# Prefill of a hybrid attention and mLSTM step: the norm half a block later, and four gated temporaries on the attention's probability tiles

## The chip, the cores and the metric

The kernel runs on one core of a Trainium2 chip. The metric is the device time of one execution in microseconds (us), the median over the runs. TensorE is called PE, VectorE DVE, ScalarE ACT, GpSimd POOL, and SyncE, whose queue issues most DMAs, SP.

## The reference, cut to what matters

One layer is applied to 128 prompt tokens and to 1024 latent tokens of width 1024. An attention group of 8 heads and an mLSTM group of 4 heads stand side by side, one output projection merges them, and a SwiGLU FFN follows. Each sub-layer begins with an RMS norm and ends in a gated addition to the residual:

```
mix = concatenate([attn_o, hm], axis=-1) @ w_out
x   = x + g1 * mix
h2  = rmsnorm(x, norm2_w) * (1 + sc2) + sh2
x   = x + g2 * (swiglu(h2, w_gu, w_down))
```

`hm` is the mLSTM's output, `g1`, `sc2`, `sh2` and `g2` come from the conditioning (one set for the prompt, one for the latents). A last RMS norm gives the two `y` outputs.

## The kernel before, in words

The 1152 tokens are 9 blocks of 128 (block 0 is the prompt), and three blocks make a chunk. Matrix products in float32 quality are made from three products of high and low parts (`whi`, `wlo` of a weight, `th`, `tl` of an activation).

The stages are: the conditioning and the input projection; the four mLSTM heads, with the attention of chunk 0 beside them; a stage called **prefill**; then the FFN of the three chunks, with the attention of the next chunk woven in beside the first products of each.

`prefill` works through the nine blocks. It multiplies the mLSTM half of `mix` with its half of `w_out` and adds the gated result to the residual. For each block `b` there are these steps:

- `mix(b)`: four transposes of the block's `hm` on PE, a copy on ACT (`th`, L1265) and a subtraction on DVE (`tl`, recorded as L141). It ends by issuing the load of `hm` of block `b + 2`.
- `half(b, n)`, for each half `n` of the 1024 columns: `out_block`, twelve 128x512 matmuls into one PSUM bank (L1219, L1221, L1223), and then `add_gated`: a multiplication of the bank with the gate on DVE into a temporary `t` (L1180), and an addition of `t` to the residual tile on POOL (L1181). Blocks 6 to 8 load `x` and store the sum instead (L1279 to L1283).
- `end(b)`: for blocks 0 to 2, `stats` (a squared sum on ACT, L1398, and a reciprocal square root in a dozen small DVE steps, L131 to L137), and, for `b` = 2, 3, 4, `norm2(0, cur, b - 2)`.

`norm2` makes the FFN's input of one block, in two halves: a scaled copy on ACT (`y`, L1414), four transposes on PE (L120), four scalings (one on ACT, L1422, three on DVE, L1424) into the tile `both`, a copy of the high part on ACT (L1429) and the low part on POOL (L141, `aTl`). `gate_up` of chunk 0 (L1435 to L1437) begins when the three blocks of chunk 0 are through this.

The temporary `t` has the tag `t2`, with three buffers, in the pool `ft`. That pool is opened after the pools of the mLSTM stage are closed. The attention's probabilities `pr` have a tag of their own with two buffers, in the pool `ap2`, which was opened before the attention of chunk 0; `both` of `norm2` uses the same tag.

PSUM banks for `mix`, `half` and `norm2` come from `bank()`: three buffers of one pool, and every fourth call the one buffer of another.

Every `yield` of `prefill` adds 0.35 to a counter, and at each full one a step of the attention of chunk 1 is issued: first the load and transposes of a block's queries, then one head after the other (scores `S` on PE, L1111; maximum on DVE, L1113; exponential into `pr` on ACT, L1114; high part `ph` on ACT, L1117; low part `pl` on DVE, L1118; two transposing DMAs; later the products with the values, L1135 and L1136). The step's PE work is tied behind the last matmul of the `half` that was issued before it:

```
with tc.issue_after(cur["gate"]), tc.issue_after(loaded["gate"]), tc.issue_after(loaded["hm"]), tc.issue_after(loaded["pe"]):
    next(att, None)
```

The order on each engine is not the program's: a scheduler places the instructions by their place in the program and by what is ready. `hot(n)` puts an instruction `n` places ahead; `norm2` stands under `hot(800)`, `stats` and the attention under `hot(200)`.

Of the kernel before, what the change touches and what calls it, by code (L numbers as in the profile page):

```python
# [8 lines left out]
F32 = mybir.dt.float32  # L9
# [10 lines left out]
P = 128  # L20
# [13 lines left out]
CB = 3  # L34
NCH = NB // CB
CT = CB * P
# [10 lines left out]
def hybrid_step(ctx: ExitStack, tc: tile.TileContext, I: dict, O: dict):  # L47
# [3 lines left out]
    dve = nc.vector  # L51
    pool = nc.gpsimd
# [3 lines left out]
    def hot(n):  # L56
        return tc.high_priority(n)

    def nm(s):
        uid[0] += 1  # L60
        return f"{s}_{uid[0]}"
# [19 lines left out]
    def xrow(b):  # L81
        if b == 0:
            return I["x_prompt"][0]
        return I["x_sample"][0, (b - 1) * P : b * P, :]
# [21 lines left out]
    def bank():  # L106
        turn_of[0] += 1
        at = psum["mm"] if "mm1" not in psum or turn_of[0] % 4 else psum["mm1"]
        return at.tile([P, 512], F32, name=nm("mm"), tag="mm")
# [9 lines left out]
    def transpose(out, in_, n=P):  # L119
        nc.tensor.transpose(out, in_, ident[:n, :n])  # L120
# [19 lines left out]
    def sub(out, full, hi, eng):  # L140
        (dve if eng == "dve" else pool).tensor_tensor(out=out, in0=full, in1=hi, op=ALU.subtract)  # L141
# [187 lines left out]
    ps = bank()  # L329
# [3 lines left out]
    ps = bank()  # L333
# [730 lines left out]
    ap2 = ctx.enter_context(tc.tile_pool(name="ap2", bufs=1, side="right", reuse_waits="tile"))  # L1064
# [88 lines left out]
    def a_tiles():  # L1153
        return (hp.tile([P, KD, CT], F32R, name=nm("aTh"), tag="b2"),
                hp.tile([P, KD, CT], F32R, name=nm("aTl"), tag="b3"))
# [18 lines left out]
    def t2():  # L1174
        return ft.tile([P, 512], F32, name=nm("t2"), tag="t2", bufs=3)

    def add_gated(x1, ps, g, n, eng=dve):
        cs = slice(n * 512, (n + 1) * 512)
        t = t2()
        dve.tensor_tensor(out=t, in0=ps, in1=g, op=ALU.mult)  # L1180
        eng.tensor_tensor(out=x1[:, cs], in0=x1[:, cs], in1=t, op=ALU.add)  # L1181

# [16 lines left out]
    def out_pieces(half, n, raw=None):  # L1199
        pieces = []  # L1200
        for j in range(2):
            r0 = half * 512 + 2 * j * P
            rows = w_out[r0 : r0 + 2 * P, n * 512 : (n + 1) * 512].rearrange("(a p) n -> p a n", p=P)
            pieces.append(load_piece([(full_view, rows)], (2, 512), raw=raw))
        return pieces

    def out_gates():
        gs = []
        for n in range(2):
            gl = xg.tile([P, 512], F32, name=nm("gl"), tag=("gl", "gx")[n], bufs=1)  # L1210
            dma(gl, g_d[0, 1:2, n * 512 : (n + 1) * 512].to_broadcast([P, 512]))
            gs.append(gl)
        return gs

    def out_block(ws, n, th, tl):
        ps = bank()
        for k in range(4):
            wh = ws[n][k // 2][0]
            mm(ps, th[:, k], wh[:, k % 2, :], start=(k == 0), stop=False)  # L1219
        for k in range(4):  # L1220
            mm(ps, th[:, k], ws[n][k // 2][1][:, k % 2, :], start=False, stop=False)  # L1221
        for k in range(4):
            loaded["pe"] = mm(ps, tl[:, k], ws[n][k // 2][0][:, k % 2, :], start=False, stop=(k == 3)).ins  # L1223
        return ps

    def prefill(cur, nxt):

        x1s = cur["x1"], nxt["x1"]
        cur["rs"] = []

        def load_hm(b):
            if b >= NB:
                return None
            hm = xe.tile([P, 512], F32, name=nm("hmr"), tag="hmr", bufs=2)
            if b < CB:
                loaded["hm"] = dma(hm, hm_d[0][b * P : (b + 1) * P, :]).ins
            else:
                r = dma(hm.rearrange("p (h n) -> p h n", n=P), hm_d[b // CB][:, :, b % CB * P : (b % CB + 1) * P])
                if b == CB:
                    loaded["hm"] = r.ins  # L1240
            return hm

        def load_x1(b):
            if CB <= b < 2 * CB:
                dma(x1s[1][b % CB], xrow(b))

        hms = hms_first
        ws = [ws_first]
        gs = out_gates()
        gx_all = xe.tile([P, D], F32, name="gx_all", tag="mx", bufs=3)  # L1250
        gate = loaded["gate"] = dma(gx_all, g_d[0, 0:1, :].to_broadcast([P, D])).ins
        ws.append(out_pieces(1, 1))
        cur["gate"] = loaded["piece"]
        gx = [gx_all[:, n * 512 : (n + 1) * 512] for n in range(2)]
        mixed = {}

        def mix(b):
            t = xe.tile([P, NQ, P], F32R, name=nm("mx"), tag="mx", bufs=3)
            th, tl = mixed[b] = t[:, 0:4], t[:, 4:8]
            hm = hms.pop(0)  # L1260
            ps = bank()
            for j in range(4):
                transpose(ps[:, j * P : (j + 1) * P], hm[:, j * P : (j + 1) * P])
            psv = ps.rearrange("p (j x) -> p j x", j=4)
            nc.scalar.copy(th, psv)  # L1265
            sub(tl, psv, th.bitcast(F32), "dve")
            with tc.issue_after(gate):
                hms.append(load_hm(b + 2))

        def half(b, n):  # L1270
            c, i = divmod(b, CB)
            cs = slice(n * 512, (n + 1) * 512)
            ps = out_block(ws, n, *mixed[b])
            g = gx[n] if b == 0 else gs[n]
            if c < 2:
                add_gated(x1s[c][i], ps, g, n, pool)
            else:
                xt = t2()
                dma(xt, xrow(b)[:, cs])  # L1279
                t = t2()  # L1280
                dve.tensor_tensor(out=t, in0=ps, in1=g, op=ALU.mult)
                pool.tensor_tensor(out=xt, in0=xt, in1=t, op=ALU.add)
                dma(x1_d[i][:, cs], xt)  # L1283

        def end(b):
            if b < CB:
                with hot(200):
                    cur["rs"] += stats(x1s[0][b : b + 1])
            if 2 <= b < CB + 2:
                yield from norm2(0, cur, b - 2)  # L1290

        for b in range(2):
            mix(b)
            yield
        for b in range(2):
            half(b, 0)
            yield
        load_x1(2)
        half(0, 1)
        yield  # L1300
        yield from end(0)
        load_x1(3)
        mix(2)
        yield
        half(1, 1)
        yield
        yield from end(1)
        for b in range(2, NB):
            load_x1(b + 2)
            half(b, 0)  # L1310
            yield
            if b + 1 < NB:
                mix(b + 1)
                yield
            half(b, 1)
            yield
            yield from end(b)

    def attn_out_first(oT, ready):

# [81 lines left out]
    def norm2(c, a, i):  # L1402

        x1 = a["x1"][i]
        if "h2" not in a:
            a["h2"] = a_tiles()
        th, tl = a["h2"]
        r = a["rs"][i]
        both = ap2.tile([P, KD, P], F32, name=nm("fl"), tag="pr", bufs=2)
        cnd = 0 if c * CB + i == 0 else 1  # L1410
        for half in range(2):
            with hot(800):
                y = fp.tile([P, 512], F32, name=nm("y"), tag="y", bufs=2)
                act(y, x1[:, half * 512 : (half + 1) * 512], AF.Copy, scale=r)  # L1414
                ps = bank()
                for j in range(4):
                    transpose(ps[:, j * P : (j + 1) * P], y[:, j * P : (j + 1) * P])
                full = both[:, half * 4 : half * 4 + 4]
                for j in range(4):
                    k = half * 4 + j  # L1420
                    if j == 0 and c == 0:
                        act(full[:, j, :], ps[:, j * P : (j + 1) * P], AF.Identity, scale=scale2[:, k, cnd : cnd + 1], bias=shift2[:, k, cnd : cnd + 1])  # L1422
                        continue
                    dve.tensor_scalar(  # L1424
                        out=full[:, j, :], in0=ps[:, j * P : (j + 1) * P],
                        scalar1=scale2[:, k, cnd : cnd + 1], scalar2=shift2[:, k, cnd : cnd + 1],
                        op0=ALU.mult, op1=ALU.add)
                oh = th[:, half * 4 : half * 4 + 4, i * P : (i + 1) * P]
                nc.scalar.copy(oh, full)  # L1429
                sub(tl[:, half * 4 : half * 4 + 4, i * P : (i + 1) * P], full, oh.bitcast(F32), "pool" if c == 0 else "dve")  # L1430
            yield True
# [141 lines left out]
    cur, nxt = {}, {}  # L1573
# [27 lines left out]
    for c in range(NCH):  # L1601
        if c + 1 < NCH:
# [17 lines left out]
            cur = nxt  # L1620
# [61 lines left out]
```

## Time and profile before

| | |
|---|---|
| time, median of 3 runs | 1529.1 us (1527.36 to 1534.01) |
| the profiled execution, own time | 1531.07 us |
| its span, first to last instruction | 1529.3 us |
| PE busy in the span | 1473.0 us (96%) |
| DVE, ACT, POOL busy | 1015.8, 770.4, 268.8 us |
| mean granted PE clock | 0.989 of full speed |
| prefill on PE, first `mix` to last `half` | 485.4 to 567.9 us |

The busy times are of one execution. What an engine does off the path that sets the end costs nothing; a stretch in which PE waits, or runs at a lower granted clock, is lost only if PE is the one that is waited for afterwards.

### The profile page before, as it was taken

What the parts mean: (1) busy time and instruction counts of PE and PEld (TensorE: products, weight loads), DVE (VectorE), ACT (ScalarE), POOL (GpSimd) and SP (SyncE); (2) the same over time, 40 slices, a digit from 0 to 9 for tenths busy, and PEclk for the clock granted to TensorE, in tenths of its full rate; (3) what the DMA queues carried; (4) which work ended last, traced back from release to release, by engine and by line L of the source; (5) the groups of instructions that cost most, each with busy time, mean ns of one, the idle gap of its engine ahead of it and who ended that gap; (6) DMA issues with size and microseconds to landing.
All of it is one profiled execution on the core that took longest, in us unless ns stands there. A gap on an engine that the chain in (4) does not pass through costs nothing.

```text
span 1529.3 us, 23410 instructions
## 1 busy us (share of the span) xinstructions
PE 1473.0 (96%) x8539; PEld 1244.7 (81%) x8539; DVE 1015.8 (66%) x2025; ACT 770.4 (50%) x1429; POOL 268.8 (18%) x354
## 2 busy tenths in 40 slices
PE   6899999999998899999999999999999999999997
PEld 3545567677766789999898999989998989999996
DVE  4887654838568866878637587787866585554554
ACT  4764475947654645556433444656553443323333
POOL 0113423333344441010010100100010101101110
PEclk9899999999999999999999999999999999999998
DMA  9664323523456577869635357886864445544541
GB/s 359 205 198 147 101 71 42 120 53 62 110 177 207 135 180 187 200 156 195 171 115 166 124 184 212 198 184 145 201 145 138 138 139 179 158 135 126 153 144 56
DMA packets 387113, 233.77 MB, mean 153 GB/s; under 512 B 170102, under 2 KB 347462, under 8 KB 386998
## 3 DMA queue, kind: packets, MB, share of 16 engines
q1 hardware_dynamic: 385006, 228.69, 55.0%
q10 hardware_dynamic: 1864, 3.20, 0.9%
q8 instruction: 67, 1.10, 0.3%
q14 instruction: 48, 0.39, 0.1%
q0 software_dynamic: 128, 0.39, 0.1%
HBM read 182.21 MB, written 11.69 MB: 127 GB/s over the span
## 4 chain that ended last, share of the span: by engine, by line
PE 78%; DVE 5%; DMA 3%; ACT 3%; issue 1%; POOL 1%; SPq 0%; ACTq 0%; DVEq 0%; POOLq 0%
PE mm L1437 11%; PE mm L1436 11%; PE mm L1435 11%; PE mm L1191 5%; PE mm L1192 5%; PE mm L1193 5%; PE S L1111 4%; PE wi L514 3%; PE wi L513 3%; PE wi L512 3%; PE mm L1219 2%; PE po L1136 2%; PE po L1135 2%; PE mm L1221 2%; PE mm L1223 2%
## 5 line engine op out<-in xcount | busy, mean ns | idle before, releaser
L163 ACT CAST whi<-raw 128x1024 fp32r<-128x1024 f32 x214 | 219.2, 1026 | 367.8 <-PE mm L1436 146.9
L141 DVE TENSOR_TENSOR wlo<-raw,whi 128x1024 fp32r<-128x1024 f32 x214 | 257.7, 1204 | 170.5 <-ACT whi L163 167.0
L1436 PE MATMUL mm<-aTl,whi 128*128 128x384 f32 x1056 | 354.4, 336 | 0.0
L1437 PE MATMUL mm<-aTh,wlo 128*128 128x384 f32 x1056 | 354.2, 336 | 0.0
L1435 PE MATMUL mm<-aTh,whi 128*128 128x384 f32 x1056 | 353.2, 335 | 0.0
L141 POOL TENSOR_TENSOR hl<-tn,hl 128x384 fp32r<-128x384 f32 x66 | 84.9, 1286 | 846.6 <-ACT hl L1458 796.4
L1435 PEld LDWEIGHTS mm<-aTh,whi 128*128 128x128 f32 x1056 | 198.3, 188 | 0.7
L1436 PEld LDWEIGHTS mm<-aTl,whi 128*128 128x128 f32 x1056 | 198.3, 188 | 0.6
L1437 PEld LDWEIGHTS mm<-aTh,wlo 128*128 128x128 f32 x1056 | 198.3, 188 | 0.1
L1191 PE MATMUL mm<-whi,hl 128*128 128x512 f32 x372 | 144.4, 392 | 1.1 <-DVE t L1180 1.1
L1192 PE MATMUL mm<-wlo,hl 128*128 128x512 f32 x372 | 145.1, 391 | 0.0
L1193 PE MATMUL mm<-whi,hl 128*128 128x512 f32 x372 | 142.7, 391 | 0.0
L1118 DVE SCALAR_TENSOR_TENSOR pl<-pr,st,ph 128x1152 f16<-128x1152 f32 (+1 forms) x72 | 96.9, 1346 | 37.3 <-ACT ph L1117 35.9
L1113 DVE TENSOR_REDUCE st<-S 128x1 f32<-128x1152 f32 (+1 forms) x72 | 88.9, 1234 | 17.5 <-PE S L1111 17.2
L1114 ACT ACTIVATE pr<-S,st 128x1152 f32<-128x1152 f32 (+1 forms) x72 | 81.3, 1129 | 33.0 <-DVE st L1113 28.2
L1117 ACT ACTIVATE ph<-pr,st 128x1152 f16<-128x1152 f32 (+1 forms) x72 | 83.8, 1164 | 26.3 <-issue 10.9
L1180 DVE TENSOR_TENSOR t<-mm,gl 128x512 f32<-128x512 f32 x102 | 69.1, 686 | 38.1 <-PE mm L1193 16.0
L512 PE MATMUL wi<-headw,hT 128*128 128x384 f16 x288 | 93.9, 326 | 0.2 <-ACT th L799 0.2
L513 PE MATMUL wi<-headw,hT 128*128 128x384 f16 x288 | 93.9, 326 | 0.0
L514 PE MATMUL wi<-headw,hT 128*128 128x384 f16 x288 | 93.9, 326 | 0.0
L1111 PE MATMUL S<-kst,qT 128*128 128x384 f32 (+1 forms) x400 | 84.5, 344 | 0.8 <-ACT pr L1114 0.8
L1191 PEld LDWEIGHTS mm<-whi,hl 128*128 128x128 f32 x372 | 69.9, 188 | 15.2 <-DVE t L1180 1.5
(400 smaller groups left out, 2591.3 us busy)
## 6 DMA issues: line engine op xcount, KB each, us to landing
raw<-in_w_gu_dram SPq DMA_DIRECT2D x132, 512.0 KB
raw<-in_w_down_dram SPq DMA_DIRECT2D x60, 512.0 KB
a<-in_w_ada_dram SPq DMA_DIRECT2D x24, 512.0 KB
gl<-g_d SPq DMA_DIRECT2D x36, 256.0 KB
aw<-in_w_ada_dram SPq DMA_DIRECT2D x16, 512.0 KB
iraw<-in_w_in_dram SPq DMA_DIRECT2D x32, 256.0 KB
x<-in_x_sample_dram SPq DMA_DIRECT2D x11, 512.0 KB
raw<-in_w_out_dram SPq DMA_DIRECT2D x10, 512.0 KB
```

The lines of the kernel that those rows point to most:

```text
L141: (dve if eng == "dve" else pool).tensor_tensor(out=out, in0=full, in1=hi, op=ALU.subtract)
L163: nc.scalar.copy(hi[:, :n], raw[:, :n])
L512: mm(ps[:, :n], ah, wh[:, k % 2, c0 : c0 + n], start=(k == 0), stop=False)
L513: mm(ps[:, :n], ah, wl[:, k % 2, c0 : c0 + n], start=False, stop=False)
L514: mm(ps[:, :n], al, wh[:, k % 2, c0 : c0 + n], start=False, stop=(k == KD - 1))
L1111: mm(S[:, n, 0:w], qT[:, h, :], kst[kv][:, t, c0 + n * w : c0 + (n + 1) * w], start=(t == 0), stop=(t == 1))
L1191: mm(ps, ah, wh[:, k % 2, :], start=(k == 0), stop=False)
L1192: mm(ps, ah, wl[:, k % 2, :], start=False, stop=False)
L1193: mm(ps, al, wh[:, k % 2, :], start=False, stop=(k == nk - 1))
L1435: mm(ps, wh[:, k, :], th[:, k, :], start=(k == 0), stop=False)
L1436: mm(ps, wh[:, k, :], tl[:, k, :], start=False, stop=False)
L1437: mm(ps, wl[:, k, :], th[:, k, :], start=False, stop=(k == KD - 1))
```

## The change

`norm2` of blocks 0, 1 and 2 moves from the end of blocks 2, 3 and 4 to the middle of blocks 3, 4 and 5: in the program it stands behind `half(b, 0)` and ahead of `mix(b + 1)` and `half(b, 1)`. `end(b)` keeps only the statistics. The number of yields is the same.

The four gated temporaries of blocks 0 and 1 no longer take the tag `t2`. For each `n`, one tile of the tag `pr` is taken, and the two blocks use its columns 0 to 511 and 512 to 1023. All later temporaries stay as they are.

```
-    def add_gated(x1, ps, g, n, eng=dve):
+    def add_gated(x1, ps, g, n, eng=dve, t=None):
         cs = slice(n * 512, (n + 1) * 512)
-        t = t2()
+        t = t2() if t is None else t
...
             if c < 2:
-                add_gated(x1s[c][i], ps, g, n, pool)
+                if b < 2:
+                    if b == 0:
+                        mixed["t", n] = ap2.tile([P, 3, CT], F32, name=nm("t2"), tag="pr", bufs=2).rearrange("p a n -> p (a n)")
+                    t = mixed["t", n][:, b * 512 : (b + 1) * 512]
+                else:
+                    t = None
+                add_gated(x1s[c][i], ps, g, n, pool, t)
...
                     cur["rs"] += stats(x1s[0][b : b + 1])
-            if 2 <= b < CB + 2:
-                yield from norm2(0, cur, b - 2)
...
-        yield from end(0)
+        end(0)
...
-        yield from end(1)
+        end(1)
         for b in range(2, NB):
             load_x1(b + 2)
             half(b, 0)
             yield
+            if 3 <= b < CB + 3:
+                yield from norm2(0, cur, b - 3)
             if b + 1 < NB:
                 mix(b + 1)
                 yield
             half(b, 1)
             yield
-            yield from end(b)
+            end(b)
```

## The prediction

> **What bounds the kernel now.** I read the page first, then the windows by stage, then who waited for whom on PE after prefill, then PE's own timeline through prefill.
>
> ```profile
> span 1529.3 us, 23410 instructions
> PE 1473.0 (96%) x8539; PEld 1244.7 (81%) x8539; DVE 1015.8 (66%) x2025; ACT 770.4 (50%) x1429; POOL 268.8 (18%) x354
> ...
> 486.00:515.00 29.00, 25.39 (x122) 20.90 (x122) 24.98 (x66) 14.90 (x27) 13.80 (x11) 1.00 0.77 227
> 515.00:526.00 11.00, 8.60 (x32) 6.66 (x31) 7.88 (x27) 8.85 (x15) 3.81 (x3) 0.69 0.43 80
> 526.00:568.00 42.00, 42.00 (x235) 34.36 (x234) 32.57 (x56) 20.71 (x31) 19.30 (x14) 1.00 0.62 148
> 568.00:1529.30 961.30, 947.24 (x5186) 879.41 (x5184) 628.65 (x912) 425.79 (x568) 86.15 (x67) 1.00 0.59 159
> ...
> PE po L1136 <- DMA plT<-pl: 1.7, 2, 1.0
> PE mm L1191 <- DVE t L1180: 1.1, 1, 1.1
> PE po L1135 <- DMA phT<-ph: 0.4, 1, 0.4
> ```
>
> The window rows give the stretch, its length, the busy time of PE, PEld, DVE, ACT and POOL with counts, the granted PE clock, the DMA share and GB/s. From 568 us to the end PE is busy for 947.24 of 961.30 us, and all its named waits there come to 1.7 + 1.1 + 0.4 = 3.2 us. So what prefill gains or loses on PE is carried to the end nearly whole. In prefill PE has lost time in two places only: before 515, and from 515 to 526, where it also ran at a granted clock of 0.69. From 526 to 568 it is full, and nothing can be gained there. Here are the losses, on PE's timeline (start, length, and in brackets the idle time before it and what ended it):
>
> ```profile
> 488.60 1.19 PE L1219 MATMUL mm<-whi,mx 128*128 128x512 f32 x4 [1.81 <-ACT mx L1265]
> ...
> 498.92 0.60 PE L120 MATMUL mm<-ident,hmr 128*128 128x128 f32 x4
> 501.12 1.20 PE L1219 MATMUL mm<-whi,mx 128*128 128x512 f32 x4 [1.61 <-DVE mx L141]
> ...
> 506.72 1.21 PE L1111 MATMUL S<-kst,qT 128*128 128x384 f32 x6
> ...
> 511.27 1.20 PE L1219 MATMUL mm<-whi,mx 128*128 128x512 f32 x4
> ...
> 514.14 1.22 PE L1111 MATMUL S<-kst,qT 128*128 128x384 f32 x6
> 517.17 1.55 PE L120 MATMUL mm<-ident,y 128*128 128x128 f32 x8 [1.82 <-ACT y L1414]
> 518.52 1.06 PE L120 MATMUL mm<-ident,hmr 128*128 128x128 f32 x4
> 520.15 2.04 PE L1219 MATMUL mm<-whi,mx 128*128 128x512 f32 x4 [0.57 <-DVE fl L1424]
> ...
> 515.00:518.00 3.00, 1.18 (x9) 1.00 0.66 80
> 518.00:525.00 7.00, 6.42 (x20) 0.51 0.39 92
> ```
>
> The last two rows are windows of PE alone. At 501.12 the block (1,1) starts 1.61 us late. At 517.17 the transposes of `norm2(0)` wait 1.82 us for `y`, and at 520.15 block (3,1) waits 0.57 us more, behind `norm2`'s scaling on DVE. PE was busy for 1.18 of the 3.00 us up to 518; then its clock stood at 0.51 until about 525, over 6.42 us of work, which costs 6.42 x (1 - 0.51) = 3.15 us. Together 1.61 + 1.82 + 0.57 + 3.15 = 7.15 us. That is what the change can reach; the 1.81 us at 488.60 wait for `mix(0)`, which it does not touch.
>
> **Why `y` was late.** The rows of DVE, POOL and ACT, and one of SP's waits (us in total, times, longest):
>
> ```profile
> 497.48 0.16 DVE L137 SCALAR_TENSOR_TENSOR ry<-rt,ry 128x3 f32<-128x3 f32 x1
> 499.11 1.36 DVE L1113 TENSOR_REDUCE st<-S 128x1 f32<-128x1152 f32 x1 [1.47 <-PE S L1111]
> ...
> 501.93 0.67 DVE L1180 TENSOR_TENSOR t<-mm,gx_all 128x512 f32<-128x512 f32 x1
> ...
> SPq L1245 <- DMA hm_d<-hm: 1.1, 1, 1.1
> ...
> 501.34 1.28 SPq L1245 DMA_DIRECT2D x<-in_x_sample_dram  x3
> ...
> 502.69 7.15 POOL L1181 TENSOR_TENSOR x1a<-x1a,t 128x512 f32<-128x512 f32 x4 [3.08 <-DVE st L1116]
> ...
> 508.63 1.06 ACT L1398 ACTIVATE jk<-x1a 128x1024 bf16<-128x1024 f32 x1 [4.61 <-POOL x1a L1181]
> ...
> 516.41 1.32 ACT L1414 ACTIVATE y<-x1a,ry 128x512 f32<-128x512 f32 x2
> ```
>
> By 498.92 PE had left three finished blocks in PSUM, yet the first gated multiplication runs at 501.93, although DVE stood idle for 1.47 us before 499.11. So it was not DVE that was missing. The load of `x` into a newly opened pool waited until 501.34 for the mLSTM's last store to land; the `t2` temporaries lie in a pool opened at the same place, and the first write to one follows 0.6 us later. I take from this that their memory came free only then (an inference: the rows show the times, not the address). From there the chain is plain: four POOL additions in 7.15 us, ACT waiting 4.61 us for them, `stats(0)` at 508.63, `y` at 516.41, PE at 517.17. The three full banks and the one of `mix(2)` are also the four that exist, which is the wait at 501.12.
>
> **The change, part by part.** No instruction is added or removed.
>
> *Temporaries.* The first three multiplications (0.67 us each) can now run when their blocks are done, from about 493 to 499, and the additions after them. The banks of blocks (0,0) and (1,0) are then free before PE asks for one at 499.5, so the 1.61 us go whole. The additions can end by about 502 instead of 502.69 + 7.15 = 509.84; `stats(0)` still writes a `t2` tile, so it cannot start before about 501.5, which is 508.63 - 501.5 = 7.1 us earlier. Then `y` is at hand near 517.17 - 7.1 = 510, while PE, 1.61 us early, would be through its scores at 513.7. The 1.82 and 0.57 us lose their cause, and with PE busy the drop in clock has none either. But the scheduler places `norm2` 800 places ahead, by its own forecast of when `y` is ready, and may put the transposes earlier as well, in front of work that is ready. I count half of 1.82 + 0.57 = 2.39 as coming back: 1.2 us.
>
> *What the additions meet instead.* POOL's additions slow DVE:
>
> ```profile
> 512.68 1.29 POOL L1181 TENSOR_TENSOR x1a<-x1a,t 128x512 f32<-128x512 f32 x1 [0.76 <-DVE rt L136]
> ...
> 512.72 1.26 DVE L137 SCALAR_TENSOR_TENSOR ry<-rt,ry 128x1 f32<-128x1 f32 x1
> ```
>
> A step of 0.16 us (497.48) took 1.26 us at 512.72, ending with POOL's addition. Four additions among DVE's last mLSTM steps could so cost 4 x 1.1 = 4.4 us of DVE; the same collisions vanish where they were, which could give about 2 us back; so -2 to +4.4, and DVE has 29.00 - 24.98 = 4.0 us idle in that stretch to take it. I take +1.0, near the idle end. The Trainium skill, "SBUF — State Buffer", section "SBUF: two separate sides", calls the port pair that DVE and GpSimd share an exclusive lock, on which the loser stops for the whole instruction; the 1.26 us agree, and the rule speaks against moving additions into a busier stretch.
>
> *The `pr` tiles.* Both are now taken until the additions of blocks (1,0) and (1,1). The attention wants them here:
>
> ```profile
> 500.51 1.22 ACT L1114 ACTIVATE pr<-S,st 128x1152 f32<-128x1152 f32 x1 [0.37 <-DVE st L1113]
> ...
> 511.20 1.22 ACT L1114 ACTIVATE pr<-S,st 128x1152 f32<-128x1152 f32 x1
> ```
>
> The first exponential (500.51) needs one, the second (511.20) the other. With additions from 494 on, the first tile is free near 499.5 and the second near 505, so this costs nothing; the bound above is in the rivals.
>
> *The norm.* Per block it is two `y` copies, eight transposes, eight scalings, two copies and two subtractions, no DMA. It is moved past one `half`: twelve matmuls of 514.14 - 511.27 = 2.87 us, one multiplication and one addition; SP's queue isn't touched, and on POOL two subtractions go behind one addition. The 511.27 block is already (3,0), so PE did it ahead of `norm2(0)` before: the move writes down the order that was run. The attention's third head is now tied behind (3,0) instead of (2,1), which it followed anyway. I cost the move at 0. Its cover is the gap to the first product that needs `norm2`:
>
> ```profile
> 540.29 2.55 POOL L141 TENSOR_TENSOR aTl<-fl,aTh 128x512 fp32r<-128x512 f32 x2 [1.55 <-ACT aTh L1429]
> ...
> 567.70 0.33 PE L1435 MATMUL mm<-aTh,whi 128*128 128x384 f32 x1
> ```
>
> The last low part ends at 542.84, the first FFN product is at 567.70: 24.9 us to spare, against half a block of some 3 us. Without that cover it would cost those 3 us.
>
> *The sum.* 7.15 - 1.2 - 1.0 = 4.95, so 5.0 us. The profiled execution took 1531.07 us (span 1529.3 and 1.8 around it), 2.0 above the median of 1529.1. It becomes 1526.1, and the median 1524.1.
>
> *The clock term.* 3.15 of the 5.0 us rest on the dip, which followed a pause of 1.82 us, while pauses of 1.81 (488.60) and 1.61 (501.12) brought none. The Trainium skill, "TensorE: Matmul & The Clock Gate", section "Part 1: The HAM clock gate", has the clock halved after an idle window of about 3.4 us, in windows that run freely. The half clock agrees (0.51), but here a stretch only 61% idle was enough. By that rule the dip hangs on the phase of such windows; without it the sum is that of the first rival.
>
> **The rivals.**
>
> 1. *The dip is not in every execution.* For it: two like pauses brought none. Against: the stretch before 518 is the emptiest of the three. Then the gain is 4.95 - 3.15 = 1.8 us: 1527.3.
> 2. *Nothing moves.* `t2` was not what held the multiplications, or the scheduler puts `y`'s transposes ahead by as much as `y` comes earlier. For it: the address isn't shown. Against: 1.47 us of idle DVE with three full banks. 1529.1.
> 3. *Slower: the first exponential waits for its tile.* If the additions stay where they are, that of (1,0) ends at about 506.2 (half of the four), and the exponential starts 5.7 us late. It decides from 506.72 - 1.3 = 505.4 on, where the second scores on PE wait for the first's exponential. At 506.2 PE waits 0.7 us; ACT, blocked until then, brings `mix(3)`'s copy about 1.5 us late and `y` another 1.1 us, and none of the 7.15 us is saved: +3.3, 1532.4. A second dip of 3.2 us would make it 1535.6. Against it: POOL was idle for 3.08 us before 502.69.
> 4. *More than the sum.* No pause comes back, the collisions cost nothing, and `mix(0)`'s 1.81 us go in the new order: 7.15 + 1.81 = 8.96, 1520.1.
>
> **How the numbers follow.** The forecast has 0.50, the rivals 0.10, 0.14, 0.18 and 0.08 in their order. A measurement of this kernel can tell about 0.5% (7.6 us) from no change. Faster by more than that needs rival 4 or the forecast's edge: 0.10. Slower by more than that (over 1536.7) needs the third with two dips or a pause in the FFN besides: 0.08. The rest, 0.82, lies within. The range goes from just below rival 4, 1519.5, past the third's 1532.4 towards its second dip: 1534.
>
> **What would show it.** Right: the first L1180 near 493 to 496, no pause before the block (1,1), `stats(0)` near 502, the clock at 1.00 from 515 to 526, and the first L1435 near 563 instead of 567.7. Wrong: L1180 still at 501.9 (second rival); the first L1114 in prefill waiting for POOL, and PE for it (third); a dip elsewhere in prefill; or pauses of PE after 568 that come to more than about 5 us.

## The result, and the profile after

The changed kernel took 1535.36 us, the median of eleven executions (1532.58 to 1537.87). The kernel before took 1530.85 in eleven executions beside it (1527.36 to 1534.23). The ratio is 1.0032, with a 95% interval of 1.0021 to 1.0043: some 4.9 us slower (4.5 us between the medians), where 5.0 us faster was forecast. The measured time lies 1.4 us above the range. The forecast of 1524.1 was counted from the first three executions' 1529.1; with eleven the kernel before stands 1.75 us higher.

The page of the kernel after, its first lines:

```profile
span 1533.2 us, 23408 instructions
...
PE 1475.9 (96%) x8539; PEld 1246.5 (81%) x8539; DVE 1020.0 (67%) x2025; ACT 770.5 (50%) x1429; POOL 271.0 (18%) x354
```

Prefill starts 3.1 us later in this profile (see below), so the three windows of the prediction are cut 3.1 us later here. The rows behind them are PE alone (busy time, granted clock, DMA share, GB/s):

```profile
489.12:518.12 29.00, 26.32 (x120) 21.72 (x120) 24.45 (x51) 14.21 (x26) 12.71 (x11) 0.94 0.63 194
518.12:529.12 11.00, 8.13 (x34) 6.69 (x33) 9.26 (x37) 8.85 (x14) 3.03 (x4) 0.69 0.82 172
529.12:571.12 42.00, 40.64 (x230) 34.16 (x229) 32.99 (x56) 21.36 (x33) 21.52 (x15) 1.00 0.56 132
...
492.42:495.83 3.41, 3.41 (x12) 0.50 0.76 211
519.73:526.56 6.83, 4.84 (x16) 0.50 1.03 217
491.72:572.01 80.29, 75.29 (x378) 0.94 0.62 152
572.01:1533.20 961.19, 947.38 (x5187) 1.00 0.60 159
```

In the second window PE is now busy for 8.13 us instead of 8.60, and its clock is no better (0.69 both times). DVE has a little more to do there, 9.26 us where it had 7.88. The third window, which could only lose, lost 1.4 us. PE's timeline after shows the places:

```profile
491.72 1.51 PE L1219 MATMUL mm<-whi,mx 128*128 128x512 f32 x4 [1.81 <-ACT mx L1265]
...
503.97 1.18 PE L1219 MATMUL mm<-whi,mx 128*128 128x512 f32 x4
...
517.51 1.33 PE L1111 MATMUL S<-kst,qT 128*128 128x384 f32 x6 [0.77 <-ACT pr L1114]
...
521.72 1.11 PE L120 MATMUL mm<-ident,y 128*128 128x128 f32 x4 [2.87 <-ACT y L1420]
...
539.96 1.19 PE L1219 MATMUL mm<-whi,mx 128*128 128x512 f32 x4 [1.36 <-DVE t L1180]
...
572.01 0.33 PE L1441 MATMUL mm<-aTh,whi 128*128 128x384 f32 x1
...
583.92 0.27 PE L1135 MATMUL po<-phT,vs 128*128 128x256 f16 x1 [1.83 <-DVE tn L1461]
```

The block (1,1) at 503.97 starts without a pause, so the bank wait of 1.61 us is gone, as forecast. The 0.57 us in front of (3,1) are gone too, and the 1.81 us at the start are as they were. The others grew or are new: the scores wait 0.77 us, `y` is waited for 2.87 instead of 1.82 us, a product at 539.96 waits 1.36 for DVE's multiplication (I take it to be for a bank), and early in the FFN the values product L1135 waits 1.83 where the only such wait before was 0.4. Later in the FFN the 1.7 us for L1136 are gone, so the named waits behind 568 come to 2.9 us, where they had come to 3.2.

Prefill starts with the first L1219 on `mx`, called A from here on: at 488.60 before and 491.72 after, which is 3.1 us of the 3.9 by which the two profiled spans differ. On every engine the order of the instructions is the same in both kernels up to there, and A lies anywhere from 486.7 to 492.5 in the profiles of this study (487.70 in e4, which has the new temporaries too; e5's profile, at a lower clock throughout, has it at 499.25). So I don't read those 3.1 us as the change's. Places are given as distances from A, and the verdicts rest on the medians.

The profiles do not show where the whole loss lies. From A to the first FFN product they take 79.1 and 80.9 us before (the first profile and that of e1, below) and 80.3 and 79.7 after (the first and that of e2); from there to the last instruction 961.6 and 960.4 before, 961.2 and 962.2 after. That is 0.7 us on average, of some 4 that the medians differ by. What the change does to the order is read from the profiles; what it costs, from the medians of the experiments.

### Why `y` did not come earlier

Rows of the kernel after, by engine (DVE, POOL, ACT), and one of SP's waits:

```profile
497.12 0.68 DVE L1180 TENSOR_TENSOR t<-mm,gx_all 128x512 f32<-128x512 f32 x1
...
501.81 0.69 DVE L1180 TENSOR_TENSOR t<-mm,gl 128x512 f32<-128x512 f32 x1 [0.89 <-DMA gl<-g_d]
...
502.61 1.28 DVE L137 SCALAR_TENSOR_TENSOR ry<-rt,ry 128x3 f32<-128x3 f32 x1
...
505.18 1.28 DVE L136 SCALAR_TENSOR_TENSOR rt<-rt,rv 128x3 f32<-128x3 f32 x1
506.57 1.35 DVE L1113 TENSOR_REDUCE st<-S 128x1 f32<-128x1152 f32 x1
```

```profile
505.15 1.29 POOL L1181 TENSOR_TENSOR x1a<-x1a,t 128x512 f32<-128x512 f32 x1 [1.28 <-DVE rt L135]
...
508.04 0.59 POOL L965 DMA_DIRECT2D hm_d<-hm  x1 [0.41 <-POOL hm L960]
...
508.01 1.22 ACT L1114 ACTIVATE pr<-S,st 128x1152 f32<-128x1152 f32 x1 [3.18 <-DVE st L1113]
...
510.28 1.26 ACT L1117 ACTIVATE ph<-pr,st 128x1152 f16<-128x1152 f32 x1 [0.48 <-DVE st L1116]
511.45 1.04 ACT L1404 ACTIVATE jk<-x1a 128x1024 bf16<-128x1024 f32 x1
...
516.15 1.22 ACT L1114 ACTIVATE pr<-S,st 128x1152 f32<-128x1152 f32 x1 [1.58 <-DVE st L1113]
...
518.76 1.26 ACT L1117 ACTIVATE ph<-pr,st 128x1152 f16<-128x1152 f32 x1 [1.29 <-DVE ry L137]
519.92 1.04 ACT L1404 ACTIVATE jk<-x1a 128x1024 bf16<-128x1024 f32 x1
...
520.96 1.32 ACT L1420 ACTIVATE y<-x1a,ry 128x512 f32<-128x512 f32 x2
```

```profile
SPq L1245 <- DMA hm_d<-hm: 3.1, 1, 3.1
```

The first multiplication comes 5.4 us behind A, where it had come 13.3 behind it. But DVE works through one queue, and now the multiplications stand in it among the last steps of the mLSTM (L131 to L137 on `128x3`) and ahead of the maximum of head 0 (L1113). The second one waits 0.89 us for its gate, with the rest of those steps behind it; two of the small steps take 1.28 us instead of 0.16 beside POOL's additions. So the mLSTM's last store is issued at 508.04, 16.3 us behind A, and SP's next load waits 3.1 us for it (1.1 before). Before, the store was 10.4 behind A:

```profile
499.03 0.58 POOL L965 DMA_DIRECT2D hm_d<-hm  x1 [0.42 <-POOL hm L960]
...
501.85 0.16 DVE L1115 RECIPROCAL st<-st 128x1 f32<-128x1 f32 x1 [0.78 <-ACT pr L1114]
...
507.97 1.35 DVE L1113 TENSOR_REDUCE st<-S 128x1 f32<-128x1152 f32 x1
...
514.21 1.26 ACT L1117 ACTIVATE ph<-pr,st 128x1152 f16<-128x1152 f32 x1 [1.71 <-DVE rt L135]
...
516.41 1.32 ACT L1414 ACTIVATE y<-x1a,ry 128x512 f32<-128x512 f32 x2
```

These are rows of the kernel before. In both kernels ACT does things in the order exponential of head 1, `ph` of head 1, statistics of block 2, `y` of block 0. Little in that chain was waiting for the temporaries: head 1's maximum ended at 507.97 + 1.35 = 509.32, and its exponential ran at 511.20, behind the statistics of blocks 0 and 1, which makes 1.9 us at most. Block 0's residual is complete at 505.15 + 1.29 = 506.44 after, ACT stands idle until 508.01, and still the statistics run at 511.45: in ACT's queue they stand behind head 0's exponential and `ph`, which wait for L1113. The places, in us behind A, from these rows and the same ones of two experiments (e6, with the tie of e5, has a profile at full clock with the places of e5: 9.1, 11.2, 15.3 and 26.5 for the first multiplication, the store, `stats(0)` and `y`):

| | before | after | tied behind the mLSTM (e5) | early gate (e7) |
|---|---|---|---|---|
| first gated multiplication | 13.3 | 5.4 | 9.1 | 4.0 |
| mLSTM's last store | 10.4 | 16.3 | 11.2 | 14.0 |
| head 0's maximum, L1113 | 10.5 | 14.9 | 11.1 | 12.5 |
| head 0's exponential, L1114 | 11.9 | 16.3 | 13.2 | 14.0 |
| `stats(0)` | 20.0 | 19.7 | 15.3 | 17.4 |
| `y` of block 0 | 27.8 | 29.2 | 26.5 | 26.9 |
| PE's wait for `y` | 1.82 | 2.87 | 1.30 | 2.91 |

### The profile page after: what moved, and what is told of

Its sections match the earlier page's. It is cut to its first block, busy times and chain, and to the rows that moved or that the text cites. A ratio compares the mean times of both kernels' runs of the same rounds, so it can differ in the third digit from the quotient of the medians.

```text
span 1533.2 us, 23408 instructions
## 1 busy us (share of the span) xinstructions
PE 1475.9 (96%) x8539; PEld 1246.5 (81%) x8539; DVE 1020.0 (67%) x2025; ACT 770.5 (50%) x1429; POOL 271.0 (18%) x354
## 4 chain that ended last, share of the span: by engine, by line
PE 61%; DVE 2%; DMA 1%; ACT 0%; issue 0%; DVEq 0%; ACTq 0%
PE mm L1443 12%; PE mm L1442 12%; PE mm L1441 12%; PE mm L1191 5%; PE mm L1192 5%; PE mm L1193 5%; PE S L1111 3%; PE po L1136 2%; PE po L1135 1%; PE mm L1219 1%; PE mm L1223 1%; PE mm L1221 1%; PE mm L120 0%; DMA raw<-in_w_gu_dram 0%; DVE fl L1430 0%; DVE t L1180 0%
## 5 line engine op out<-in xcount | busy, mean ns | idle before, releaser
L1114 ACT ACTIVATE pr<-S,st 128x1152 f32<-128x1152 f32 (+1 forms) x72 | 81.3, 1129 | 45.0 <-DVE st L1113 40.4
L1113 DVE TENSOR_REDUCE st<-S 128x1 f32<-128x1152 f32 (+1 forms) x72 | 88.9, 1235 | 15.6 <-PE S L1111 15.1
L1180 DVE TENSOR_TENSOR t<-mm,gl 128x512 f32<-128x512 f32 x102 | 69.3, 687 | 41.7 <-PE mm L1193 15.3
```

## The experiments

My theory after the result: the multiplications, now free to go early, go ahead of the mLSTM's last steps in DVE's queue and hold up everything behind them. Its rivals: the `pr` tiles hold up the attention; the norm's move does it; the two kernels differ by chance. The times below are medians of twelve executions (five for e8), each with its ratio to runs of the kernel before on the same chip.

**e1 and e2, both kernels again.** No edit.

> The kernel before, unchanged, for a second profile. In the first pair of profiles the first prefill product starts at 488.60 us before and at 491.72 after, though the order of instructions on every engine is the same up to there. If that 3.1 us is chance, this profile starts it anywhere between 488 and 492, and first prefill product to first FFN product takes 79 us again (78 to 80). Time equal to before within 0.2%.

> The changed kernel, unchanged, for a second profile. If the loss lies in prefill, first prefill product to first FFN product takes 82 to 84 us in this profile, against 80.3 in the first one; if part of it lies ahead of prefill in every execution, the first prefill product starts near 491.7 again. Time 4 to 5 us above before.

Before: 1530.25 us, 0.9994 [0.9982, 1.0005]. After: 1534.61 us, 1.0024 [1.0012, 1.0037]. The loss is real. The second profile of after has the pauses of the first, 1.21 us for `pr`, 2.88 for `y` and 1.35 for DVE's multiplication, and one more of 0.90; the second multiplication waits 2.11 us for its gate. But both expectations of the stretch from A to the first FFN product failed: 80.9 us in e1 instead of 78 to 80, and 79.7 in e2 instead of 82 to 84. In e1 a dip right behind A puts every place 1.6 us later (the store 12.0, `stats(0)` 21.6, `y` 29.4), so `y` is no later in after than in that profile of before. PE's wait for it, 1.80 us there, is the steadier mark.

**e3 and e4, each part alone.** e3 is after without the `pr` temporaries; e4 is before with them.

> Only the norm is moved; the temporaries stay on t2. Theory N (the norm is at fault: its two halves are drawn apart on ACT and DVE, and PE waits between them): 4 to 5 us slower than before, with pauses of PE in front of the second and third block's transposes. Theory T (the temporaries are at fault: the gated work goes ahead of the mLSTM's last steps and of the first head in DVE's queue, and the statistics stay behind that head on ACT): within 1.5 us of before.

> Only the four temporaries go onto the pr tiles; the norm stays at the end of the block. Theory T: 4 to 5 us slower than before, the statistics of block 0 again some 20 us after the first prefill product, and the last store of the mLSTM output some 4 to 6 us later than before. Theory N: within 1.5 us of before, or faster by the 1.6 us of PE's wait for a bank.

The norm alone: 1532.85 us, 1.0015 [1.0002, 1.0028]. The temporaries alone: 1534.57 us, 1.0020 [1.0007, 1.0033]. Both lose. With the temporaries alone the early part is that of after (store 15.9 us behind A, `y` 28.8, waited for 2.89 us). With the norm alone it is that of before (store 10.4, `y` 27.8), and the pauses come behind it; PE's timeline of e3, and the waits of its FFN:

```profile
504.98 1.20 PE L1219 MATMUL mm<-whi,mx 128*128 128x512 f32 x4 [1.61 <-DVE mx L141]
521.06 0.66 PE L120 MATMUL mm<-ident,y 128*128 128x128 f32 x4 [2.29 <-ACT y L1414]
534.71 1.20 PE L1219 MATMUL mm<-whi,mx 128*128 128x512 f32 x4 [0.64 <-DVE t L1180]
```

```profile
PE po L1135 <- DMA phT<-ph: 1.8, 1, 1.8
```

The wait for `y` is 2.29 instead of 1.82 us, a new one of 0.64 follows where the 0.57 are gone, and L1135 waits 1.8 instead of 0.4. So moving the norm alone, which I costed at 0, costs about 2 us (0.3 to 4.3 by the interval), more than theory T and less than theory N had for it.

**e5 and e6, the multiplications tied behind the mLSTM.** The same freedom, but not past its last small step:

```
-            dve.scalar_tensor_tensor(out=y, in0=t, scalar=1.5, in1=y, op0=ALU.add, op1=ALU.mult)
+            loaded["rsqrt"] = dve.scalar_tensor_tensor(out=y, in0=t, scalar=1.5, in1=y, op0=ALU.add, op1=ALU.mult).ins
...
+        scan_last = loaded["rsqrt"]
...
-                add_gated(x1s[c][i], ps, g, n, pool, t)
+                with tc.issue_after(scan_last) if b < 2 else nullcontext():
+                    add_gated(x1s[c][i], ps, g, n, pool, t)
```

The third of these lines stands at the start of `prefill`, so it names the last such step of the mLSTM. e5 is after with it, e6 is e4 with it.

> The changed kernel, with the four gated multiplications of blocks 0 and 1 tied behind the last DVE step of the mLSTM's last reciprocal square root. Theory Q (on DVE's queue the multiplications went ahead of the mLSTM's last steps, waited there for the gate's load and met POOL's additions, so that the first head and the statistics behind them came no earlier): the last mLSTM store is back at 10.4 us after the first prefill product instead of 16.3, the statistics of block 0 start at 14 to 17 us instead of 19.7, y at 22 to 26 instead of 29.2, and PE's wait of 2.9 us for it is gone or under 1 us: 2 to 5 us faster than the changed kernel, 1527 to 1533. Rival P (the pr tiles themselves hold the attention up): as slow as the changed kernel, with the first or second exponential waiting for POOL.

> The same tie, with the norm at the end of the block as before. Theory Q: 2 to 5 us faster than the temporaries alone (which took 1534.6), so at or below before. If the move of the norm costs 1.5 us by itself, as the run with the norm alone may say, this one is 1 to 2 us faster than the one with both.

e5: 1530.68 us, 1.0004 [0.9990, 1.0017]. e6: 1532.87 us, 1.0010 [0.9999, 1.0021]. The profiled execution of e5 had a granted clock of 0.95 from end to end outside its dips, so its span (1539.3 us) is not read, only its places (DVE, POOL, ACT, PE), which e6's profile at full clock repeats:

```profile
508.15 0.16 DVE L137 SCALAR_TENSOR_TENSOR ry<-rt,ry 128x3 f32<-128x3 f32 x1
508.34 0.69 DVE L1180 TENSOR_TENSOR t<-mm,gx_all 128x512 f32<-128x512 f32 x1
509.13 0.69 DVE L1180 TENSOR_TENSOR t<-mm,gl 128x512 f32<-128x512 f32 x1
509.74 0.68 DVE L1180 TENSOR_TENSOR t<-mm,gx_all 128x512 f32<-128x512 f32 x1
510.33 1.35 DVE L1113 TENSOR_REDUCE st<-S 128x1 f32<-128x1152 f32 x1
...
510.47 0.59 POOL L965 DMA_DIRECT2D hm_d<-hm  x1
...
512.42 1.23 ACT L1114 ACTIVATE pr<-S,st 128x1152 f32<-128x1152 f32 x1 [1.65 <-POOL x1a L1181]
...
523.88 1.33 PE L1111 MATMUL S<-kst,qT 128*128 128x384 f32 x6 [1.24 <-ACT pr L1114]
526.52 1.12 PE L120 MATMUL mm<-ident,y 128*128 128x128 f32 x4 [1.30 <-ACT y L1422]
```

The three multiplications stand as a block behind the last small step, which takes 0.16 us again, and the store goes out at once. `stats(0)` is 15.3 us behind A and `y` 26.5. With the norm moved, putting the order in DVE's queue right takes the loss of after away; with the norm in its old place the tie's gain (e6 on e4) is within the intervals, so there it is not shown. Theory Q had more: `y` at 22 to 26 us behind A, PE's wait for it under 1 us (1.30 here), and e6 at or below before. The rows show one thing more: here the first exponential does wait for POOL's addition (1.65 us), and PE for it (1.24 us). That is the price of the `pr` tiles from the third rival; in after it was hidden behind L1113.

**e7, the gate at hand.** Two tiles of the tag `ph` hold the gate of block 1 from the start of prefill, so that no multiplication waits for it; otherwise after:

```
+        for n in range(2):
+            g1.append(ap2.tile([P, 512], F32, name=nm("g1"), tag="ph", bufs=2))
+            dma(g1[n], g_d[0, 1:2, n * 512 : (n + 1) * 512].to_broadcast([P, 512]))
...
-            g = gx[n] if b == 0 else gs[n]
+            g = gx[n] if b == 0 else g1[n] if b == 1 else gs[n]
```

> The changed kernel, with a second copy of the latents' gate for block 1, loaded into two ph tiles that are free long before, so that the second multiplication needn't wait for the late load. The order on PE, ACT and POOL is that of the changed kernel, and on DVE nearly. Theory Q: DVE's wait of 0.9 and 2.1 us for the gate is gone, the mLSTM's last store comes about 1 to 2 us earlier than at 16.3 us after the first prefill product, and y as much earlier than at 29.2; total 1 to 2 us faster than the changed kernel. If the order alone does it, there is no difference over 0.5 us.

1533.73 us, 1.0018 [1.0003, 1.0032], which can't be told from after. PE's timeline and two rows of DVE:

```profile
514.39 0.66 PE L120 MATMUL mm<-ident,y 128*128 128x128 f32 x4 [2.91 <-ACT y L1424]
...
493.89 0.69 DVE L1180 TENSOR_TENSOR t<-mm,g 128x512 f32<-128x512 f32 x1
494.69 1.28 DVE L133 TENSOR_SCALAR ry<-rh 128x3 int32<-128x3 int32 x1
```

The gate wait was worth 2.3 us of the store (14.0 instead of 16.3 us behind A) and `y` came 2.3 us earlier. Yet PE waits 2.91 us for it, because it stood at the transposes 2.3 us sooner: the pause for `pr` went (0.77 us), and after's early dip of 1.7 us is not in this profile. An earlier `y` did not shorten the wait; what PE has in front of its transposes counts as much.

**e8, the temporaries elsewhere.** `t = ap2.tile([P, 512], F32, name=nm("t2"), tag=("ph", "pl")[n], bufs=2)` in place of the halves of a `pr` tile.

> The changed kernel, with the four temporaries on four tiles of the tags ph and pl, so that both pr tiles are free for the attention. Theory Q: the same as the changed kernel within 1 us, with y some 29 us after the first prefill product. Rival P: the scores' waits of 0.8 to 1.2 us for the exponential vanish and the kernel is 1 to 3 us faster.

1535.75 us, 1.0038 [1.0026, 1.0050]: as slow as after, with no `pr` tile taken. The early part is that of after (store 16.2 us behind A, `y` 30.6), and PE waits 1.96 us for the exponential and 3.67 us for `y`. The first two exponentials wait for DVE's maxima (4.51 and 1.26 us), not for a tile. The `pr` tiles are not the cause of after's loss.

**e9 and e10, the fourth weight copy of the FFN.** In after, `ph` of the last head stands behind one more weight copy on ACT than its exponential does, and the values product at the FFN's start waits. Here the copy is tied behind it; e9 is e3 with this, e10 is e5 with it:

```
-                    act(phv, prv, AF.Copy, scale=st[:, 3:4])
+                    loaded["ph"] = act(phv, prv, AF.Copy, scale=st[:, 3:4]).ins
...
-                    wh, wl = load_piece([(full_view, src)], (KD, P))
+                    loaded["ffn"] = loaded.get("ffn", 0) + 1
+                    with tc.issue_after(loaded["ph"]) if loaded["ffn"] == 4 else nullcontext():
+                        wh, wl = load_piece([(full_view, src)], (KD, P))
```

> The norm alone moved (1532.9 before this edit), with one weight copy of the FFN, the fourth, tied on ACT behind the high part ph of head 7. In every run but the kernel before, that copy stands between head 7's exponential and its ph, and waits there for a weight load. Theory C (that order makes PE wait 1.8 us for the transposed probabilities at the start of the FFN): the wait falls to 0.5 us or less and the kernel gets 1 to 2 us faster, to before within 1 us. Rival W (the wait there is filled by something else PE would have to wait for, the copied weight itself): another wait of 1 to 2 us in the FFN's first 20 us and no gain.

> The changed kernel with both ties: the multiplications behind the mLSTM's last step on DVE, and the fourth weight copy behind head 7's ph on ACT. Theory C with theory Q: 1 to 2 us faster than the first tie alone (1530.7, ratio 1.0004), so 1529 to 1530 and 1 to 2 us faster than before. Rival W: equal to the first tie alone.

e9: 1532.35 us, 1.0016 [1.0002, 1.0030]. e10: 1531.61 us, 1.0002 [0.9987, 1.0017]. Both are where they were without it. ACT's rows of e9, and a wait of PE:

```profile
568.49 1.22 ACT L1114 ACTIVATE pr<-S,st 128x1152 f32<-128x1152 f32 x1 [4.65 <-DVE st L1113]
...
570.27 1.26 ACT L1117 ACTIVATE ph<-pr,st 128x1152 f16<-128x1152 f32 x1 [0.47 <-ACT pr L1114]
```

```profile
PE po L1135 <- DVE tn L1457: 2.1, 1, 2.1
```

`ph` now follows its exponential at once, and PE waits 2.1 us all the same. The copy was not the cause.

**e11 and e12, the norm's place on PE tied down.** In the program `norm2` goes behind `half(b, 1)`, and its transposes are tied behind the last matmul issued before them; e11 is after with this, e12 is e10 with it:

```
-            if 3 <= b < CB + 3:
-                yield from norm2(0, cur, b - 3)
             if b + 1 < NB:
...
             half(b, 1)
             yield
+            if 3 <= b < CB + 3:
+                yield from norm2(0, cur, b - 3)
...
-                for j in range(4):
-                    transpose(ps[:, j * P : (j + 1) * P], y[:, j * P : (j + 1) * P])
+                with tc.issue_after(loaded["pe"]) if c == 0 else nullcontext():
+                    for j in range(4):
+                        transpose(ps[:, j * P : (j + 1) * P], y[:, j * P : (j + 1) * P])
```

> The changed kernel with the norm's place really enforced: norm2 stands behind half(b, 1) of blocks 3 to 5 and its transposes are tied on PE behind that half's last matmul. If the place of the transposes on PE is what costs the 2.9 us (the place in the program alone did not move them), PE does block (3,1) first, 2.9 us of work, and the wait for y falls under 0.5 us: 2 to 3 us faster than the changed kernel. If y gets later by as much as PE does other work (ACT and DVE being the ones that are late), the wait stays over 1.5 us and the time is that of the changed kernel.

> All three ties together. Each mends one wait: no wait for y over 0.5 us, no wait at the FFN's start over 0.5 us, the last mLSTM store at 11 us after the first prefill product. The waits that before had in prefill are 1.6, 1.8 and 0.6 to 0.9 us, and each clock dip costs 1.7 us: 3 to 6 us faster than before, 1525 to 1528, if nothing new comes up; within 1 us of before if PE then waits for ACT or DVE in other places of prefill.

e11: 1530.98 us, 1.0000 [0.9989, 1.0011], so the tie alone takes after back to the time before. Its profile does not show how. PE does block (3,1) first, but `y` comes later (30.4 us behind A instead of 29.2) and PE still waits 1.62 us for it, which by the expectation should have left the time at that of after; and PE's idle time from A on, 19.3 us, is as long as after's (18.8 and 20.9).

e12: 1527.31 us (1524.41 to 1530.46), 0.9978 [0.9967, 0.9990], some 3.4 us faster than before: the one version that beats both kernels. PE's timeline of e12 has these rows, the second of which is its only pause of note between the first and the last product of prefill; the third lies in the FFN:

```profile
518.35 0.66 PE L120 MATMUL mm<-ident,y 128*128 128x128 f32 x4
...
523.23 1.19 PE L1219 MATMUL mm<-whi,mx 128*128 128x512 f32 x4 [0.61 <-DVE mx L141]
...
576.59 0.27 PE L1135 MATMUL po<-phT,vs 128*128 128x256 f16 x1 [2.31 <-ACT whi L163]
```

```profile
515.00:526.00 11.00, 10.25 (x52) 8.28 (x51) 10.90 (x37) 8.06 (x16) 3.87 (x3) 1.00 0.60 134
...
578.02:581.43 3.41, 3.41 (x19) 0.50 0.80 232
```

The first row has all engines, the second PE alone.

The first transposes of `y` come 27.8 us behind A, earlier than after's 30.0, and wait for nothing: in front of them stands a block that PE can already do. Prefill, from A to the first FFN product, takes 72.1 us (79.1 and 80.9 before, 572.01 - 491.72 = 80.3 and 79.7 after), and no dip falls into it. About half of that gain is paid back behind it: L1135 waits 2.31 us, against the 0.5 us at most that were expected, a dip follows, and from the first FFN product to the end it takes 965.0 us, where before took 961.6 and 960.4.

The ties make a square of four kernels: after has neither (1.0032 and 1.0024), e5 and e10 the tie on DVE (1.0004 and 1.0002), e11 the tie on PE (1.0000), e12 both (0.9978). Each tie takes 0.22 to 0.28% off, with or without the other. So the loss does not hang on one place alone, and what both ties mend goes beyond it. Whether the tie on PE would gain as much on the kernel before, without the freed temporaries, no run shows.

**Where the time went, over the profiles.** Prefill is taken from A to the first FFN product; what is behind it, to the last instruction. PE idle is what PE's busy time leaves of the stretch; a dip costs the busy time multiplied by (1 - clock), over windows of 1 us. All in us.

| | prefill | PE idle, prefill | PE idle, behind it | dips, ahead of prefill | dips, in prefill | ratio of the times |
|---|---|---|---|---|---|---|
| before; e1 | 79.1; 80.9 | 4.1; 4.5 | 14.1; 12.9 | 8.9; 6.6 | 3.1; 4.6 | 1; 0.9994 |
| after; e2 | 80.3; 79.7 | 5.0; 6.3 | 13.8; 14.6 | 9.7; 8.0 | 4.1; 1.7 | 1.0032; 1.0024 |
| e3, norm alone | 78.1 | 4.9 | 14.4 | 11.6 | 1.7 | 1.0015 |
| e4, temporaries alone | 79.6 | 5.9 | 16.6 | 6.8 | 1.4 | 1.0020 |
| e6, e4 tied | 78.7 | 5.0 | 15.4 | 11.8 | 1.7 | 1.0010 |
| e7, early gate | 77.3 | 4.3 | 14.6 | 6.5 | 1.7 | 1.0018 |
| e8, other tiles | 81.3 | 7.1 | 14.9 | 8.2 | 2.4 | 1.0038 |
| e9, e3 and copy | 77.4 | 5.7 | 14.6 | 8.2 | 0.0 | 1.0016 |
| e10, e5 and copy | 78.0 | 2.6 | 14.3 | 11.6 | 4.6 | 1.0002 |
| e11, norm tied | 77.8 | 3.8 | 15.5 | 6.6 | 1.6 | 1.0000 |
| e12, all three | 72.1 | 0.8 | 15.8 | 8.1 | 0.0 | 0.9978 |

Behind prefill only e7 and e12 have a dip that costs PE time, 1.7 us each. Idle time of PE from A on is 17.8 us before (mean of two) and 19.9 after, a difference of 2.1 us of the 3.4 to 4.9 that the times differ by. It goes with the ratios only roughly: e12 and e10 have the least (16.6 and 16.9), e8 and e4 the most (22.0 and 22.5), but e6 (20.4, 1.0010), e11 (19.3, 1.0000) and after's first profile (18.8, 1.0032) do not fit. The other 1 to 3 us I could not place. After's two profiles differ by more than that in their dips alone (13.8 and 9.7 us), and the dips of an execution without a profile aren't seen.

## Why the prediction was wrong

- *The first multiplications near 493 to 496, and the bank wait gone.* Right: 497.12, which is 5.4 us behind A instead of 13.3, and no pause at (1,1). That the tile decides is borne out by e3 (13.3 with `t2`) and e4 (3.9 without), and the rival "nothing moves" fell. That the memory came free only near 501.3 is not shown: before, the first multiplication follows L1115 in DVE's queue, which waited until 501.85 for head 0's exponential.
- *"`stats(0)` still writes a `t2` tile, so it cannot start before about 501.5, which is 508.63 - 501.5 = 7.1 us earlier."* This is the step that failed. I moved the additions and left all else where it was, the mLSTM's last store above all. But the multiplications took places in DVE's queue ahead of that store's last steps and of head 0. `stats(0)` came 0.3 us earlier by distance from A (19.7 instead of 20.0; 19.8 in e2). In e5, where the mLSTM goes first, it came 4.7 of the 7.1 us earlier.
- *"Then `y` is at hand near 517.17 - 7.1 = 510."* This fails even with `stats(0)` early. `y` stands on ACT behind head 1's exponential and, in before and after, its `ph`. In e5 `stats(0)` came 4.7 us earlier and `y` only 1.3. So 1.82 + 3.15 us of the sum had no ground: PE waits 2.87 us for `y`, and the dip is there still (4.84 x 0.50 = 2.4 us, from 519.73). The 0.57 us did go, but 0.77 and 1.36 us came in other places.
- *The collisions with POOL, taken at 1.0 of -2 to +4.4.* Two small steps lost 1.1 us each on the path of the store, 2.2 in all: within the bounds, and too low. The cover that I named, 4.0 us of idle DVE, was none, because the loss is in the order and not in the busy time: DVE was no busier in that stretch after (24.45 of 29.00 us) than before (24.98).
- *The norm's move at 0.* Wrong by about 2 us when it is moved alone (e3: 1.0015); with the tie on DVE the move shows no cost (e5 1.0004, e6 1.0010). Its cover was there: the first FFN product at 572.01 waits for nothing. The claim that failed is that the move "writes down the order that was run". The order still follows from what is ready, not from the line in the program, and it came out another way further on. With the place tied down (e11) the wait for `y` fell to 1.62 us and after lost nothing against before.
- *The slower rival.* It named the `pr` tiles, and e8 shows that they were not what cost. That its 1535.6 with a second dip is near the measured 1535.36 is luck. Its mechanism exists (1.24 us of PE in e5) but lay behind a longer wait in after. The mechanism that decided, early work in front of a late stage's last steps in an engine's queue, was among neither the rivals nor the costs, although the prediction counted the steps that it would meet.
- *The chances.* "Within 0.5%" had 0.82, and that is where the ratio of 1.0032 lies. The sign of the forecast was wrong, so the chance came true without its reasons.

Left open: the wait of L1135 early in the FFN, 0.4 us or less in the kernel before and 1.1 to 2.4 in each variant. Neither the copy's order nor the norm's place removes it. Open too is where e11's gain lies, and where 1 to 3 us of the loss lie.

## What to carry to other kernels

Where a buffer holds work back, ask what that work will stand in front of once it is free, on each engine that issues in order: work that is early but not urgent, and waits itself for a load, can hold up the end of the stage before it. Taking away a cause of lateness is only a gain if nothing else on the way is as late; walk the queue of each engine between the freed work and the waiting one, here ACT's, and read the next latest step. And in an order that a scheduler makes, the line in the program is a wish; a tie states it, and the tie that put ready work ahead of a late operand (e11, e12) gained what earlier data (e7) did not.

## What was not expected of the hardware

The granted clock falls to 0.50 for 3.41 us at a time, or for a multiple of that. After's dip at 492.42 is one such piece, with PE busy all through: 3.41 x (1 - 0.50) = 1.7 us, and those in the prefill of e3, e6 and e7 cost 1.7 each. The Trainium skill, "TensorE: Matmul & The Clock Gate", section "Part 1: The HAM clock gate", has the clock halved in windows of about 3.4 us; the traces agree.

They also show why a like pause is followed by a dip in one profile and by none in another: it depends on how the pause falls between such windows. Cut into steps of 3.41 us from the start of a dip, the window 489.01 to 492.42 in after holds the whole of `mix(0)`'s 1.81 us, PE is busy for 1.50 us of it, and the dip follows. In before, the same 1.81 us are split at 487.31 between two windows with 2.82 and 2.12 us of work, and none follows. Over all profiles but e5's, from 60 to 1515 us, the clock fell after every window at full clock in which PE was busy for under 42%, and after none in which it was busy for over 56%; in between, either happened (1.45 us of work in before's window at 156.21 and full clock behind it, 1.89 in e11's at 485.16 and half clock behind it). Where the windows lie changes from profile to profile: A is at 488.60 and 488.56 in the two profiles of before, and the later dip starts at 518.03 and 519.96.

Ahead of prefill, where the kernels before and after have the same order of instructions, the dips cost from 6.6 to 9.7 us in their four profiles. One pair of profiles can't attribute 3 us in this kernel, and the term of 3.15 us that I took from one dip was of that size.
